# Stores on ScalarE's DMA queue, one tile late, in a batched outer-product kernel

## The chip, the cores and the metric

The kernel runs on one core of a Trainium2 chip. The metric is the device time of one execution in microseconds (us). Engines are named as in the profile: PE is the tensor engine's matmul, PEld its weight load, DVE is VectorE, ACT is ScalarE, POOL is GpSimd, SP is SyncE. A q behind the name (SPq, ACTq) is that engine's sequencer, which among other things issues DMAs.

## The reference

```
x: [8, 12, 512, 64] f32,  y: [8, 12, 512, 64] f32
out = einsum('bhtc,bhsc->bhts', x, y)      # [8, 12, 512, 512] f32
```

For each of the 96 pairs of batch and head, a 512 x 64 matrix is multiplied by the transpose of another. 25.17 MB are read and 100.66 MB written.

## The kernel before

**Tiling.** The 96 heads form NG = 12 groups of 8. A group's x and y are loaded as two transfers of 1 MB each into the two halves of one slot, a tile of 128 partitions by 16 KB; the pool has SLOTS = 5 of these. An output tile is 128 partitions by 8 x 512 f32, 2 MB, and takes a slot of the same pool. There are 4 x 12 = 48 output tiles ("results" 0 to 47), each stored by one 2 MB transfer.

**Steps.** `load(g)` takes a slot and issues the two loads on SP. `compress(g)` casts the group to bf16 into tiles that are kept: all of x on ACT, y in four quarters, of which two go to DVE, one to POOL and the last to ACT. After this the slot is free. `mix(i)` rearranges x of half a group into one of two tiles that were set to zero once, and `transposes(i)` makes the two matmul operands of that half with DVE's 32 x 32 transposes. `result(o)` takes a slot, runs eight matmuls into three PSUM tiles (of 3, 3 and 2 banks), and copies them into the slot: the first two on ACT, the third on DVE. It then records a piece of work for a later result (a `transposes` after an even result; after an odd one, a `mix` for one of the half-groups 6 to 23, with one quarter of it on ACT; half-groups 0 to 5 are mixed on POOL in the first loop), and returns a function that issues the store.

**Order.** The order is written out by hand: on each engine the instructions stand as the program calls them. The first loop runs over the 12 groups. It casts each group as its load lands, issues the remaining loads (group 10 after group 6 is cast, group 11 after group 8), and fits in results 0, 1 and 2 after groups 5, 7 and 9, whose store functions it only collects. After the loop, all 12 groups are cast. The program then calls the three collected stores, and goes on with results 3 to 47, storing each at once.

**Queues.** All loads and all stores are issued by SP, in program order: the 24 loads first, the 48 stores behind them. Each issue waits on SP for what it needs: a load for its slot to be free, a store for the copies on ACT and DVE. Since SP does nothing else, it is free to wait. It issues store 0 right after the last load, at 54.14 us, while ACT is still casting groups 9 to 11 until 65.94 us.

Of the kernel before, what the change touches and what calls it, by code (L numbers as in the profile page):

```python
# [1 line left out]

# [4 lines left out]


@with_exitstack
def kernel(  # L10
    ctx: ExitStack,
    tc: tile.TileContext,
    x: bass.AP,
    y: bass.AP,
    out: bass.AP,
):

    nc = tc.nc
    B, H, T, C = x.shape
    _, _, S, _ = y.shape
    P = 128  # L30
    G = 8
    Q = P // G
    R = T // Q
    NG = B * H // G
    K = 8
    E = R // K
    D = 32
    SLOTS = 5
    fp32 = mybir.dt.float32
    bf16 = mybir.dt.bfloat16  # L40
    u32 = mybir.dt.uint32
    COPY = mybir.ActivationFunctionType.Copy
    assert C == 2 * D and S == T and R == D and Q * 2 == D

    xv = x.rearrange("b h t c -> (b h t c)").rearrange("(g p n) -> g p n", p=P, n=R * C)
    yv = y.rearrange("b h t c -> (b h t c)").rearrange("(g p n) -> g p n", p=P, n=R * C)
    ov = out.rearrange("b h t s -> (b h t s)").rearrange(
        "(o u h q n) -> o h q u n", u=2, h=2, q=Q * E, n=K * S
    )

    const = ctx.enter_context(tc.tile_pool(name="const", bufs=1))
    kept = ctx.enter_context(tc.tile_pool(name="kept", bufs=NG))
    slots = ctx.enter_context(tc.tile_pool(name="slots", bufs=SLOTS))
    tpool = ctx.enter_context(tc.tile_pool(name="tpool", bufs=3))
    pm3pool = ctx.enter_context(tc.tile_pool(name="pm3psum", bufs=2, space=bass.MemoryType.PSUM))
    pm2pool = ctx.enter_context(tc.tile_pool(name="pm2psum", bufs=1, space=bass.MemoryType.PSUM))

    loaded, inputs, mixed, made = {}, {}, {}, {}
    zeroed = [const.tile([P, K * E * D], u32, name=f"xb{half}") for half in range(2)]
    in_front = [nc.vector, nc.gpsimd, nc.vector, nc.scalar]  # L60
    behind = [nc.vector, nc.gpsimd, nc.scalar, nc.vector]
    FIRST = NG // 2

    def copy(engine, dst, src):
        if engine is nc.scalar:
            nc.scalar.activation(dst, src, COPY)  # L66
        else:
            engine.tensor_copy(dst, src)  # L68

    def slot():  # L70
        return slots.tile([P, K * S], fp32, name="slot")

    def load(g):
        both = slot()
        nc.sync.dma_start(both[:, :R * C], xv[g])  # L75
        nc.sync.dma_start(both[:, R * C:], yv[g])
        loaded[g] = both

    def compress(g):

        both = loaded.pop(g)
        xk = kept.tile([P, R, C], bf16)
        nc.scalar.activation(xk.rearrange("p r c -> p (r c)"), both[:, :R * C], COPY)  # L83
        inputs[g] = xk
        ys = both[:, R * C:].rearrange("p (r c) -> p r c", c=C)
        for half in range(2):
            yb = kept.tile([P, R // 2 * D], u32, name=f"yb{half}")
            yv2 = yb.bitcast(bf16).rearrange("p (j c w) -> p j w c", j=R // 2, w=2)
            for ch in range(2):
                copy(  # L90
                    in_front[2 * half + ch],
                    yv2[ch * 64:(ch + 1) * 64],
                    ys[half * 64:(half + 1) * 64, :, ch * D:(ch + 1) * D].rearrange(
                        "p (j w) c -> p j w c", w=2
                    ),
                )
            mixed[2 * g + half] = yb

    def mix(i, engines, halves=(0, 1)):

        g, half = divmod(i, 2)
        xk = inputs[g]
        xv2 = zeroed[half].bitcast(bf16).rearrange("p (k e c u) -> p k e c u", k=K, e=E, u=2)
        for ch in halves:
            for u in range(2):
                lo = half * 64 + u * D
                copy(
                    engines[2 * ch + u],
                    xv2[(2 * ch + u) * D:(2 * ch + u + 1) * D, :, :, :, u],
                    xk[lo:lo + D, :, ch * D:(ch + 1) * D].rearrange("p (e k) c -> p k e c", k=K),  # L110
                )

    def transposes(i):
        xb, yb = zeroed[i % 2], mixed.pop(i)
        xT = tpool.tile([P, K * D * E], u32)
        nc.vector.transpose(  # L116
            xT.rearrange("p (k r e) -> p k e r", k=K, e=E),
            xb.rearrange("p (k e c) -> p k e c", k=K, e=E),
        )
        yT = tpool.tile([P, D * R // 2], u32)  # L120
        nc.vector.transpose(  # L121
            yT.rearrange("p (r j) -> p j r", r=D), yb.rearrange("p (j c) -> p j c", c=D)
        )
        made[i] = (xT.bitcast(bf16).rearrange("p (k h m) -> p k h m", k=K, h=2), yT.bitcast(bf16))

    def result(o):

        i, h = divmod(o, 2)
        xT, yT = made[i]
        otf = slot()  # L130
        ot = otf.rearrange("p (r s) -> p r s", s=S)
        for k, n in ((0, 3), (3, 3), (6, 2)):
            pm = (pm3pool if n == 3 else pm2pool).tile([P, n, S], fp32, name=f"pm{n}")
            for j in range(n):
                nc.tensor.matmul(  # L135
                    pm[:, j, :], xT[:, k + j, h, :], yT[:, h * S:(h + 1) * S], start=True, stop=True
                )
            copy(nc.scalar if n == 3 else nc.vector, ot[:, k:k + n, :], pm)
        if h == 0 and i + 2 < 2 * NG:
            transposes(i + 2)  # L140
        elif h == 1 and FIRST <= i + 4 < 2 * NG:
            mix(i + 4, behind)
        return lambda: nc.sync.dma_start(ov[i, h], otf)  # L143

    with tc.manual_schedule():
        for g in range(SLOTS):
            load(g)
        nc.vector.memset(zeroed[0], 0.0)  # L148
        nc.gpsimd.memset(zeroed[1], 0.0)  # L149
        stores = []  # L150
        for g in range(NG):
            compress(g)
            mix(g // 2, [nc.gpsimd] * 4, (g % 2,))
            if g in (2, 4):
                transposes(g // 2 - 1)
            if g < 5:
                load(g + SLOTS)
            elif g in (5, 7, 9):
                stores.append(result(len(stores)))
            elif g in (6, 8):  # L160
                load(g // 2 + 7)
        for store in stores:
            store()
        for o in range(len(stores), 4 * NG):
            result(o)()


# [1 line left out]
_INS = ['x', 'y']  # L169
_OUTS = [((8, 12, 512, 512), 'float32')]  # L170


# [23 lines left out]
```

## Time and profile before

| | us |
|---|---|
| median of 3 runs (301.9 to 302.25) | 301.96 |
| the profiled execution | 302.28 |
| its span, first to last instruction | 300.5 |
| DVE busy | 189.2 |
| ACT busy | 198.1 |
| PE busy | 148.4 |
| POOL busy | 82.0 |
| one store issue on SP, median of 48 | 0.539 |
| ACT waiting for a store to land, 33 times | 51.3 |

The profile page describes one execution on the chip. A row of the list of groups reads: line, engine, operation, output<-input with shapes, count; then busy time in all and mean ns of one; then idle time of the engine just before, and what ended it. The strip cuts the span into 40 slices of 7.5 us; each digit is a busy share in tenths. "DMA to landing" is the time from an issue's start until its data has arrived and the semaphore says so. A line of the timeline reads: start, duration, engine, line, operation. Matmul ends are modelled. An engine's idle time costs nothing unless the end of the program hangs on it.

### The profile page before, as it was taken

Reading aid. Unit: us, or ns where it says so; the run is one execution under the profiler, and the core shown is the slowest. Engines: PE = TensorE matmul, PEld = TensorE weight load, DVE = VectorE, ACT = ScalarE, POOL = GpSimd, SP = SyncE. Lnnn points to the kernel's source line nnn. Section 1 sums busy time; section 2 is a strip of 40 time slices with the busy share of each in tenths; the row PEclk is TensorE's granted clock in tenths of the full one; section 3 lists DMA queues with packets and bytes.
Section 4 is the critical chain, followed back from the end, with each engine's and each line's share of the span. In section 5 each row is a group of like instructions: output and inputs, shape, how many; then the busy total and the mean of one; then the engine's idle time right before and its main releaser. Section 6 shows DMA issues by size and latency. Waiting matters only on the chain.

```text
span 300.5 us, 1448 instructions
## 1 busy us (share of the span) xinstructions
PE 148.4 (49%) x384; PEld 47.6 (16%) x384; DVE 189.2 (63%) x157; ACT 198.1 (66%) x139; POOL 82.0 (27%) x59
## 2 busy tenths in 40 slices
PE   0004044228647573765675567666476767475000
PEld 0001011003212121221121122212121222121000
DVE  1568998895997669666767576757765775313000
ACT  4666598999976867686668676777677664647000
POOL 1899989991211011101110111011101100000000
PEclk9999575577997659567756855756955765955555
DMA  7999999999999999999999999999999999999994
GB/s 282 429 424 421 423 422 422 423 435 434 423 434 426 425 438 430 425 443 421 433 436 425 432 430 425 438 430 423 442 423 430 441 421 430 432 422 427 436 425 181
DMA packets 10377, 125.93 MB, mean 419 GB/s; under 512 B 1152, under 2 KB 1152, under 8 KB 1152
## 3 DMA queue, kind: packets, MB, share of 16 engines
q1 hardware_dynamic: 10368, 125.83, 98.7%
q8 instruction: 3, 0.05, 0.1%
q14 instruction: 6, 0.05, 0.0%
HBM read 25.17 MB, written 100.66 MB: 419 GB/s over the span
## 4 chain that ended last, share of the span: by engine, by line
DMA 65%; ACT 15%; DVE 7%; PE 3%; issue 1%; ACTq 1%; SPq 0%; DVEq 0%
DMA out_dram<-slot 56%; ACT slot L66 11%; DMA slot<-in_y_dram 9%; DVE yb L68 4%; PE pm L135 3%; ACT xk L83 3%; DVE xT L116 2%; ACT yb L66 2%; DVE slot L68 1%; DVE yT L121 1%; ACTq L191 0%; SPq L75 0%; ACTq L66 0%; DVEq L68 0%; SPq L143 0%
## 5 line engine op out<-in xcount | busy, mean ns | idle before, releaser
L135 PE MATMUL pm<-yT,xT 128*128 128x512 bf16 x384 | 148.4, 537 | 127.3 <-ACT slot L66 102.2
L66 ACT ACTIVATE slot<-pm 128x1536 f32<-128x1536 f32 x96 | 133.9, 1448 | 65.8 <-DMA out_dram<-slot 51.3
L68 DVE COPY slot<-pm 128x1024 f32<-128x1024 f32 x48 | 58.8, 1225 | 72.0 <-PE pm L135 54.4
L68 POOL COPY xb<-xk 32x1024 bf16<-32x1024 bf16 x42 | 62.2, 1482 | 145.4 <-DVE xT L116 144.3
L135 PEld LDWEIGHTS <-xT 128*128 128x128 bf16 x384 | 47.6, 124 | 227.2 <-issue 193.9
L116 DVE STREAM_TRANSPOSE xT<-xb 128x1024 uint32<-128x1024 uint32 x24 | 49.3, 2054 | 0.7
L68 DVE CAST yb<-slot 64x1024 bf16<-64x1024 f32 x24 | 35.2, 1466 | 13.5 <-DMA slot<-in_y_dram 13.2
L83 ACT ACTIVATE xk<-slot 128x2048 bf16<-128x2048 f32 x12 | 22.9, 1910 | 9.6 <-DMA slot<-in_x_dram 9.4
L68 DVE COPY xb<-xk 32x1024 bf16<-32x1024 bf16 x36 | 26.3, 731 | 0.5
L121 DVE STREAM_TRANSPOSE yT<-yb 128x512 uint32<-128x512 uint32 x24 | 25.0, 1041 | 0.0
L66 ACT ACTIVATE xb<-xk 32x1024 bf16<-32x1024 bf16 x18 | 24.1, 1338 | 0.4
L68 POOL CAST yb<-slot 64x1024 bf16<-64x1024 f32 x12 | 18.8, 1567 | 8.1 <-DMA slot<-in_y_dram 7.4
L66 ACT ACTIVATE yb<-slot 64x1024 bf16<-64x1024 f32 x12 | 15.9, 1324 | 3.6 <-DMA slot<-in_y_dram 3.4
L83 ACT ACT_TABLE_LOAD x1 | 1.3, 1283 | 0.7 <-PEq L180 0.7
L148 DVE MEMSET xb<- 128x1024 uint32 x1 | 0.9, 912 | 1.0 <-PEq L180 1.0
L149 POOL MEMSET xb<- 128x1024 uint32 x1 | 1.0, 952 | 0.3 <-POOLq L180 0.3
L180 POOL MEMSET const-float32-0.0<- 128x1 f32 x1 | 0.1, 98 | 0.2 <-issue 0.2
L180 POOL MEMSET const-float32-1.0<- 128x1 f32 x1 | 0.1, 98 | 0.0
L180 POOL MEMSET const-bfloat16-1.0<- 128x1 bf16 x1 | 0.1, 98 | 0.0
L180 POOL MEMSET const-uint8-127<- 128x1 uint8 x1 | 0.1, 98 | 0.0
## 6 DMA issues: line engine op xcount, KB each, us to landing
out_dram<-slot SPq DMA_DIRECT2D x48, 2048.0 KB, 21.7
slot<-in_x_dram SPq DMA_DIRECT2D x12, 1024.0 KB, 17.5
slot<-in_y_dram SPq DMA_DIRECT2D x12, 1024.0 KB, 19.3
```

Of the source, the lines that this page charges most:

```text
L66: nc.scalar.activation(dst, src, COPY)
L68: engine.tensor_copy(dst, src)
L83: nc.scalar.activation(xk.rearrange("p r c -> p (r c)"), both[:, :R * C], COPY)
L116: nc.vector.transpose(xT.rearrange("p (k r e) -> p k e r", k=K, e=E), xb.rearrange("p (k e c) -> p k e c", k=K, e=E),)
L121: nc.vector.transpose(yT.rearrange("p (r j) -> p j r", r=D), yb.rearrange("p (j c) -> p j c", c=D))
L135: nc.tensor.matmul(pm[:, j, :], xT[:, k + j, h, :], yT[:, h * S:(h + 1) * S], start=True, stop=True)
L148: nc.vector.memset(zeroed[0], 0.0)
L149: nc.gpsimd.memset(zeroed[1], 0.0)
L180: nc = _bacc.Bacc("TRN2", target_bir_lowering=False, num_devices=1)
```

## The change

The stores are issued by ACT instead of SP, and each one stands behind the copies of the next result. In detail:
- In `result`, the returned function calls `nc.scalar.dma_start` in place of `nc.sync.dma_start`.
- After the loop over the groups, stores 0 and 1 are called, and store 2 is kept back. Each further result is recorded first, with its two copies and, after an odd result, its quarter of a mix on ACT, and then the store of the result before it is called. The last store is called at the end.

On ACT, stores 0 and 1 now stand behind the casts of group 11 and ahead of the copies of result 3. SP issues the 24 loads and nothing else. No copy, matmul or transpose is added, removed or moved against another.

```diff
@@ -140,7 +141,7 @@
             transposes(i + 2)
         elif h == 1 and FIRST <= i + 4 < 2 * NG:
             mix(i + 4, behind)
-        return lambda: nc.sync.dma_start(ov[i, h], otf)
+        return lambda: nc.scalar.dma_start(ov[i, h], otf)
 
     with tc.manual_schedule():
         for g in range(SLOTS):
@@ -159,10 +160,13 @@
                 stores.append(result(len(stores)))
             elif g in (6, 8):
                 load(g // 2 + 7)
-        for store in stores:
-            store()
-        for o in range(len(stores), 4 * NG):
-            result(o)()
+        done = len(stores)
+        while len(stores) > 1:
+            stores.pop(0)()
+        for o in range(done, 4 * NG):
+            stores.append(result(o))
+            stores.pop(0)()
+        stores.pop()()
```

## The prediction

> **What bounds the kernel now.** I read the strip of 40 slices and the queues first, then the chain, then the few microseconds in which the kernel turns from loading to storing.
>
> ```profile
> DMA  7999999999999999999999999999999999999994
> GB/s 282 429 424 421 423 422 422 423 435 434 423 434 426 425 438 430 425 443 421 433 436 425 432 430 425 438 430 423 442 423 430 441 421 430 432 422 427 436 425 181
> q1 hardware_dynamic: 10368, 125.83, 98.7%
> DMA 65%; ACT 15%; DVE 7%; PE 3%; issue 1%; ACTq 1%; SPq 0%; DVEq 0%
> L66 ACT ACTIVATE slot<-pm 128x1536 f32<-128x1536 f32 x96 | 133.9, 1448 | 65.8 <-DMA out_dram<-slot 51.3
> out_dram<-slot SPq DMA_DIRECT2D x48, 2048.0 KB, 21.7
> ```
>
> The 16 DMA engines are busy in every slice but the first and last. One queue carries all 125.83 MB and fills 98.7% of the span. ACT, at 66%, waits for stores to land, not the other way round. The chain names compute engines for a third of the span, but a chain follows releases: under those pieces the strip still shows DMA at 9. So the test of the change is one question: **do the DMA engines stay fed?** Every microsecond in which they stand dry comes out at the end.
>
> A store takes 21.7 us to land, but two tiles together take 9.89 us (ACT's copies of every second tile start at 206.44 and 216.33), 4.94 each: about four stores are queued at any time. A late store is therefore harmless wherever several others are queued. The place to look is where none can be: the end of the loads.
>
> ```profile
> L76 SPq DMA_DIRECT2D slot<-in_y_dram x1: 423/423/423, 53.7 to 53.7; - x1
> DMA to landing us min/median/max: 9.1/9.1/9.1
> ...
> L143 SPq DMA_DIRECT2D out_dram<-slot x1: 653/653/653, 54.1 to 54.1; - x1
> DMA to landing us min/median/max: 13.6/13.6/13.6
> ```
>
> The last load (the y of group 11) is issued at 53.67 (timeline of SP) and lands at 62.8. Store 0 is issued at 54.14, straight behind it, and lands at 67.7, just 4.9 us, one store's time, after that load. No gap at all: before's stores 0 and 1 lie in the queue while the last loads still move, and store 2 joins at 59.4.
>
> ```profile
> 61.33 1.32 ACT L66 ACTIVATE yb<-slot 64x1024 bf16<-64x1024 f32 x1
> 62.68 1.91 ACT L83 ACTIVATE xk<-slot 128x2048 bf16<-128x2048 f32 x1
> 64.62 1.32 ACT L66 ACTIVATE yb<-slot 64x1024 bf16<-64x1024 f32 x1
> ...
> L66 ACTq EVENT_SEMAPHORE  x1: 17/17/17, 62.8 to 62.8; - x1
> ```
>
> The last two ACT rows are group 11: its x cast starts at 62.68, its y cast at 64.62. The fourth line is the first wait of ACT's sequencer (ACTq) for the copies of result 3, which follow that y cast in program order. It stands at 62.8, exactly when y of group 11 lands, and not at 65.94, when the cast ends. The same is seen for group 9: its y lands at 32.97 + 19.9 = 52.87, its cast starts only at 55.18, and the sequencer's next wait is recorded at 52.9. So ACT's sequencer passes a cast as soon as the cast's own semaphore has come.
>
> **What the Trainium skill says.** "DMA: Bandwidth & Descriptors", section "Issuing engines are not separate DMA queues": the issuing engine changes nothing but who spends the issue time; all DMAs share the same 16 engines. The trace of before has one queue at 98.7%, so it can't test this, but it leaves no bandwidth for a second queue to find. "Perfetto Trace Analysis", section "Per-engine timelines": an ACT instruction is pushed into a wait queue and the sequencer goes on, while a DMA instruction is executed by the sequencer itself. The two readings at 62.8 and 52.9 agree, with the limit that the sequencer stood still until the last pushed instruction's semaphore came. The first-named page, section "Latency and other measured facts", gives about 0.6 us to the first byte on this path; the trace's only DMA on an empty queue took longer (below).
>
> **The change part by part.**
>
> Removed: the 48 store issues on SP and SP's waits for them. SP has nothing else to do then. Worth 0.
>
> Loads: same issues and waits on SP, and in before no store stands ahead of a load. 0.
>
> Added to ACT: 48 issues, 0.54 us each on SP (538 ns the least, 653 the longest, of 48). In two tiles ACT has four copies of 1.45 and one mix of 1.34, 7.1 us of 9.89, so 2.8 are free; two issues take 1.1. Not on the path: 0. If that cover is gone, see rival C.
>
> Stores issued later: store o-1 goes out once the sequencer has passed the copies (and on every second tile the mix) of tile o. Tile o starts copying when store o-5 has landed. At that moment o-4, o-3 and o-2 are still queued, 3 x 4.94 = 14.8 us of work less the landing lag. Store o-1 follows at most 2.9 + 1.34 + 0.54 = 4.8 us later, with 2 us until it moves: some 8 us are left. 0 in the steady part and at the end; the time from issue to landing should fall by 4 us or so, which is not time saved. The added wait, for VectorE's copy of tile o-1, holds back ACT's copies of tile o+1. But in before VectorE's copy ends at 202.93 and ACT's copies of that tile at 204.27; one tile later it is long done. 0.
>
> **Stores 0 and 1: the price.** In the built order of ACT, both stand behind the casts of group 11 and ahead of the copies of result 3, and carry no semaphore wait. They can't be issued before the y cast of group 11 is passed, and that needs the last load to have landed. So the DMA engines, which run loads and nothing else until then, fall dry once:
> - last byte to landing. The first load is issued at 0.74, its packets begin at 2.7 (windows of 0.1 us: share 0.00 up to 2.70, then 0.89), it lands 4.9 after issue at 5.6, and loads land 2.48 apart (ACT's first x and y casts, 5.64 and 8.13, start on landings). 4.9 - 2.0 - 2.5 = 0.4 us.
> - landing to issue: the sequencer's wait at 62.80 against 62.77: 0.03 us.
> - issue to first packet: 2.0 us by that first load, 0.6 by the skill's figure. I take 2.0: it is measured here, and ACT's queue will be as unused as SP's was. The first load was cold in other ways too, so both ends stay: 0.6 to 2.0.
>
> Sum 0.4 + 0.0 + 2.0 = **2.4 us**, at the low end 1.0. Upwards, the mixed stretch of loads and stores is lost as well (438 GB/s in 60 to 62 us against 423 before): at most 0.3 us; and slower engines may start later: up to 3.2 in all. Is there a second dry spell? Store 1 follows 0.6 us behind store 0; together 9.9 us of work from about 64.8 to 74.7. Store 2 needs only that the copies of result 3 be passed (they start at 65.96 in before) and goes out by 68. Store 3 by about 71, behind copies that end at 71.9 in before. No.
>
> Nothing can win the time back, since the rest is DMA at 430 GB/s to the end. The profiled run took 302.28 for a span of 300.5; with 2.4 it becomes 304.7, span 302.9. The median of the runs lies 0.3 lower, at 301.96: forecast **304.4 us**.
>
> **The rivals.**
> - A: ACT issues a DMA only when its engine has finished what stands before it. Then store 0 waits for the y cast's end, 65.96 instead of 62.80: 3.2 more, 5.6 in all, 307.5. For it: no trace here shows a DMA on ACT. Against: the reading at 62.8, and store 3 on carry a semaphore wait for ACT's own copies, which would be idle if the order held by itself.
> - B, the other side, not slower: stores on a queue of their own, three deep instead of four, move faster. 100.66 MB at 430 GB/s are 234 us; the dry 2.4 us are paid back from 434.4 GB/s on. The skill's ceiling, 435 ("DMA: Bandwidth & Descriptors", "Bandwidth"), allows 231.4, so at best 301.7. For it: single slices reach 443. Against: the mean is the same in all of the store phase and nothing in it waits for the queue. A dry spell of only 0.6 us or less, below what can be seen, falls here too.
> - C: issuing from ACT costs much more than from SP, so that ACT becomes the bound. It decides from 1.4 us an issue (2.8 free over two); at 2.0 it costs 1.2 us for each of some 21 pairs, 25 us: about 329. Against: nothing in the issue itself, the same form of DMA, points to triple the price.
>
> **How the numbers follow.** Forecast 0.63, A 0.17, B 0.15, C 0.05. The range, 302.4 to 307.8, covers the forecast's 303.0 to 305.2 and A and the edge of B; it leaves C and most of B out. What can be told from no change is 0.2%, 0.6 us. B splits into 0.07 faster and 0.07 the same; 0.86 slower.
>
> **What would show it.** In the changed profile: the strip's DMA row dips in one slice around 60 to 68 us; the stores' queue shows some 80% and the loads' 20%; store 0 is issued near 62.8 and lands near 70.1 (67.7 before); the median from issue to landing drops to 17 or 18 us; ACT's waits for stores do not grow; GB/s after 70 us are 430 again. A is right if store 0 goes out at 66. The prediction is wrong if the DMA row shows no dip, if there are several, or if the rate after 70 us has moved by more than 0.5%.

## The result, and the profile after

The changed kernel takes 304.37 us (304.36 to 304.45), against 302.11 us for the kernel before beside it: a ratio of 1.0073, interval 1.0057 to 1.0088. It is 2.3 us slower. The profiled execution took 304.38 us with a span of 302.6, 2.1 us more than before in both.

From the page of the changed kernel: the strip's DMA row and rate, the queues, the first lines of the chain, ACT's copies with their idle time, and the stores' issues.

```profile
DMA  7999999979999999999999999999999999999996
GB/s 289 423 427 419 421 428 418 421 323 416 435 426 416 429 435 420 431 431 425 422 435 425 418 435 422 425 435 419 426 435 425 418 444 414 425 438 422 422 442 266
q10 hardware_dynamic: 6912, 100.67, 78.4%
q1 hardware_dynamic: 3456, 25.17, 20.1%
DMA 73%; ACT 9%; DVE 6%; PE 2%; issue 1%; ACTq 1%; SPq 0%; DVEq 0%
L67 ACT ACTIVATE slot<-pm 128x1536 f32<-128x1536 f32 x96 | 134.0, 1448 | 67.9 <-DMA out_dram<-slot 58.7
out_dram<-slot ACTq DMA_DIRECT2D x48, 2048.0 KB, 19.2
```

One digit in 40 has changed in the middle of the DMA row: the ninth slice, 60.5 to 68.1 us, is at 7 with 323 GB/s. The loads (q1) and the stores (q10) now have a queue each, and their shares add to 98.5%, of a longer span.

The next lines are from the timeline of ACT around the turn from loads to stores (start, duration, engine, line), followed by the first store's issue with its time to landing, and by windows of the same stretch. The last three figures of a window are the PE clock, the DMA share and GB/s; a packet is counted in the window in which it begins.

```profile
62.60 1.91 ACT L84 ACTIVATE xk<-slot 128x2048 bf16<-128x2048 f32 x1
62.74 2.66 ACTq L144 DMA_DIRECT2D out_dram<-slot  x3
64.53 1.33 ACT L67 ACTIVATE yb<-slot 64x1024 bf16<-64x1024 f32 x1
65.88 1.45 ACT L67 ACTIVATE slot<-pm 128x1536 f32<-128x1536 f32 x1
...
L144 ACTq DMA_DIRECT2D out_dram<-slot x1: 645/645/645, 62.7 to 62.7; - x1
DMA to landing us min/median/max: 6.8/6.8/6.8
```

```profile
62.00:64.00 2.00, 0.00 (x0) 0.00 (x0) 1.97 (x2) 1.98 (x2) 1.94 (x2) 1.00 0.00 0
64.00:66.00 2.00, 0.00 (x0) 0.00 (x0) 1.99 (x2) 1.95 (x3) 1.94 (x2) 0.71 1.14 475
80.00:290.00 210.00, 118.69 (x316) 38.78 (x320) 128.98 (x113) 137.15 (x99) 22.45 (x17) 0.72 1.01 427
```

From 62 to 64 us no packet of data begins. The last load lands at 62.7 (issued at 53.6, 9.1 to landing), ACT's sequencer issues store 0 at 62.74, while the x cast of group 11 is still running and its y cast has not begun, and packets appear at 64.0. Store 0 lands at 62.74 + 6.8 = 69.5 us, 1.8 us later than before (67.7). The kernel before had 455 GB/s in the same two microseconds:

```profile
62.00:64.00 2.00, 0.00 (x0) 0.00 (x0) 1.97 (x2) 1.98 (x2) 1.94 (x2) 1.00 1.07 455
80.00:290.00 210.00, 124.80 (x323) 39.67 (x320) 128.63 (x113) 136.29 (x99) 22.52 (x17) 0.67 1.01 430
```

At the other end, the last store lands at 280.4 + 21.4 = 301.8 us, against 278.3 + 21.4 = 299.7. From store 0's landing to the last one's are 232.3 us in the changed kernel and 232.0 in the one before, which is alike within the rounding of these figures. So nearly all of the loss is there before the store phase begins.

### The profile page after: what moved, and what is told of

Its sections match the earlier page's. It is cut to its first block, busy times and chain, and to the rows that moved or that the text cites. A ratio compares the mean times of both kernels' runs of the same rounds, so it can differ in the third digit from the quotient of the medians.

```text
span 302.6 us, 1418 instructions
## 1 busy us (share of the span) xinstructions
PE 142.7 (47%) x377; PEld 46.8 (15%) x384; DVE 189.6 (63%) x157; ACT 198.2 (66%) x139; POOL 81.9 (27%) x59
## 3 DMA queue, kind: packets, MB, share of 16 engines
q1 hardware_dynamic: 3456, 25.17, 20.1%
HBM read 25.17 MB, written 100.66 MB: 416 GB/s over the span
## 4 chain that ended last, share of the span: by engine, by line
DMA 73%; ACT 9%; DVE 6%; PE 2%; issue 1%; ACTq 1%; SPq 0%; DVEq 0%
DMA out_dram<-slot 64%; DMA slot<-in_y_dram 9%; ACT slot L67 5%; DVE yb L69 4%; ACT xk L84 2%; PE pm L136 2%; ACT yb L67 1%; DVE xT L117 1%; ACTq L144 1%; DVE slot L69 1%; DVE yT L122 1%; SPq L76 0%; ACTq L67 0%; DVEq L69 0%; ACT xb L67 0%
## 5 line engine op out<-in xcount | busy, mean ns | idle before, releaser
L136 PE MATMUL pm<-yT,xT 128*128 128x512 bf16 x377 | 142.7, 524 | 134.1 <-ACT slot L67 109.2
L67 ACT ACTIVATE slot<-pm 128x1536 f32<-128x1536 f32 x96 | 134.0, 1448 | 67.9 <-DMA out_dram<-slot 58.7
L69 POOL COPY xb<-xk 32x1024 bf16<-32x1024 bf16 x42 | 62.1, 1479 | 147.3 <-DVE xT L117 146.1
L136 PEld LDWEIGHTS <-xT 128*128 128x128 bf16 x384 | 46.8, 122 | 229.5 <-issue 194.0
## 6 DMA issues: line engine op xcount, KB each, us to landing
out_dram<-slot ACTq DMA_DIRECT2D x48, 2048.0 KB, 19.2
slot<-in_y_dram SPq DMA_DIRECT2D x12, 1024.0 KB, 19.2
```

The costliest lines, as they stand in the source:

```text
L136: nc.tensor.matmul(pm[:, j, :], xT[:, k + j, h, :], yT[:, h * S:(h + 1) * S], start=True, stop=True)
```

## The experiments

Theory D is that of the prediction: the loss is the one dry spell of the DMA engines where the loads end. Rival Q is that the loss is spread over the store phase, because of ACT's queue, the late issue, or fewer stores in flight. In all diffs below, the function that `result` returns takes the queue as an argument (ACT's if none is given).

### 1. Stores 0 and 1 back on SP

```diff
         while len(stores) > 1:
-            stores.pop(0)()
+            stores.pop(0)(nc.sync)
```

> Stores 0 and 1 are issued by SP behind the loads, as in the kernel before; all others by ACT, one tile late, as in the changed kernel. Theory D (the loss is the one dry spell of the DMA engines at the end of the loads): no dry spell, 302.2 us, and store 0 lands near 67.7. Rival Q (the loss is spread over the store phase: the ACT queue, the late issue, or the shorter queue costs about 0.05 us a store): 46 of the 48 stores still pay, 304.3 us.

Measured: 301.72 us (ratio to the kernel before 0.9982, 0.9975 to 0.9989). Two of 48 stores moved back, and all of the loss is gone. Store 0 lands at 67.7 again, and the engines are fed in the two microseconds that were dry:

```profile
62.00:64.00 2.00, 0.00 (x0) 0.00 (x0) 1.97 (x2) 1.98 (x2) 1.94 (x2) 0.50 1.06 451
```

Q falls. That the time is even 0.5 us under the kernel before was not expected; experiments 7 to 10 are about that.

### 2. The mirror image: three stores on ACT, 45 on SP

```diff
         for o in range(done, 4 * NG):
             stores.append(result(o))
-            stores.pop(0)()
-        stores.pop()()
+            if o == done:
+                stores.pop(0)()
+            stores.pop(0)(nc.sync)
```

> The mirror image: stores 0, 1 and 2 are issued by ACT behind the casts of group 11, as in the changed kernel; stores 3 to 47 by SP, each as soon as it is ready. Theory D: the dry spell from 62.0 to 64 us is there, 304.4 us, although 45 stores are issued as before. Rival Q: 302.2 us.

Measured: 304.47 us (1.0074, 1.0059 to 1.0089), as D said. The dry stretch is there again:

```profile
62.00:64.00 2.00, 0.00 (x0) 0.00 (x0) 1.96 (x3) 1.98 (x2) 1.94 (x2) 0.50 0.04 16
```

With three late stores the whole loss is back, and it doesn't matter that the other 45 are issued as before.

### 3. Only store 2 on SP

```diff
-        while len(stores) > 1:
+        stores.pop(2)(nc.sync)
+        while stores:
             stores.pop(0)()
         for o in range(done, 4 * NG):
             stores.append(result(o))
-            stores.pop(0)()
+            if o > done:
+                stores.pop(0)()
```

> The changed kernel, with store 2 alone moved to SP, where it is issued when its copies are done, near 59.4 us, ahead of stores 0 and 1. Theory D: one queued store of 4.9 us covers the spell until stores 0 and 1 come at 62.7, so no dry slice and 302.2 us. Rival Q, or a cost of being late of stores 0 and 1 themselves: 304.3 us.

Measured: 301.69 us (0.998, 0.9969 to 0.999). Stores 0 and 1 go out as late as in the changed kernel, at 62.9 us, and it costs nothing, since store 2 was issued at 59.4 and fills the engines meanwhile (414 GB/s from 62 to 64 us). So what costs is not that a given store is late but that nothing at all is queued.

### 4. The dry spell made longer

```diff
         done = len(stores)
+        for o in range(done, done + 2):
+            stores.append(result(o))
         while len(stores) > 1:
             stores.pop(0)()
-        for o in range(done, 4 * NG):
+        for o in range(done + 2, 4 * NG):
```

> The changed kernel, with stores 0, 1 and 2 placed behind the copies of result 4 (with store 3), where ACT's sequencer passes near 70.3 us instead of 62.7. Theory D: the dry spell grows by 7.5 us and comes out at the end one for one, 311.9 us. Rival R (a dry spell is partly won back, since more copies are done ahead when the stores start): under 310 us.

Measured: 311.86 us (1.0317, 1.03 to 1.0334). From the windows of this run, and its first store:

```profile
64.00:66.00 2.00, 0.00 (x0) 0.00 (x0) 1.99 (x2) 1.95 (x3) 1.94 (x2) 0.50 0.00 0
66.00:68.00 2.00, 0.58 (x2) 0.26 (x2) 2.00 (x2) 2.00 (x2) 1.94 (x2) 0.50 0.00 0
68.00:70.00 2.00, 2.00 (x7) 0.56 (x5) 0.23 (x1) 1.68 (x2) 0.31 (x1) 0.50 0.00 0
...
L144 ACTq DMA_DIRECT2D out_dram<-slot x1: 644/644/644, 70.2 to 70.2; - x1
...
DMA to landing us min/median/max: 6.9/6.9/6.9
```

The engines stand dry until past 71 us. Store 0 is issued 7.5 us later than in the changed kernel (70.25 against 62.74), and the time is 7.5 us longer: one for one, though result 3 had been copied and result 4 begun by the time the stores went out. Nothing is won back: from there on the DMA engines are the bound again, and ACT only waits longer for stores (64.2 us in all against 58.7).

### 5. Stores 0 and 1 between the two casts of group 11

```diff
         inputs[g] = xk
+        if g == NG - 1:
+            stores.pop(0)()
+            stores.pop(0)()
```

(The rest of this diff is cut: the list `stores` is made before `compress`, and the two stores are no longer called after the loop.)

> The changed kernel, with stores 0 and 1 moved on ACT from behind the y cast of group 11 to between its x cast and its y cast. ACT's sequencer passes the x cast when that x has landed, near 60.3 us. Theory D: store 0 is issued at 60.4, its packets can start at 61.7, no dry spell, 301.7 to 302.2 us. Rival A (a DMA on ACT goes out only when the engine has finished what stands before it, the x cast at 64.5): still over 306 us.

Measured: 301.87 us (0.9984, 0.9977 to 0.9991). The timeline of ACT in this run:

```profile
59.46 1.91 ACT L86 ACTIVATE xk<-slot 128x2048 bf16<-128x2048 f32 x1
60.38 1.29 ACTq L149 DMA_DIRECT2D out_dram<-slot  x2
61.40 1.33 ACT L67 ACTIVATE yb<-slot 64x1024 bf16<-64x1024 f32 x1
62.76 1.91 ACT L86 ACTIVATE xk<-slot 128x2048 bf16<-128x2048 f32 x1
```

In the program the two issues stand behind the x cast of group 11, the last line. They go out at 60.38, 2.4 us before that cast starts and while the one of group 10 is running: when x of group 11 has landed (issued at 53.3, 7.0 us to landing). This shows at a second place the rule that the forecast rested on, and it is also the cheapest repair of the changed kernel: the same queue, with the two issues moved ahead by one instruction.

### 6. The dry spell without any DMA on ACT

```diff
-        while len(stores) > 1:
-            stores.pop(0)()
+        late, stores = stores, []
         for o in range(done, 4 * NG):
-            stores.append(result(o))
-            stores.pop(0)()
-        stores.pop()()
+            result(o)(nc.sync)
+            for store in late:
+                store(nc.sync)
+            late = []
```

> No DMA on ACT at all: every store is on SP, as in the kernel before, but store 3 stands ahead of stores 0, 1 and 2, so that SP waits with all of them until the copies of result 3 end, near 68.8 us. Theory D: a dry spell from 62.0 to some 70.0 us, 6.1 us longer than in the changed kernel, 310.5 us. Rival (the loss has to do with ACT's queue): about 302 us, since all 48 stores are on SP.

Measured: 310.37 us (1.0265, 1.0251 to 1.0279). The first store is issued at 68.65 us, 5.9 later than in the changed kernel, and the time is 6.0 longer. From the windows of this run:

```profile
66.00:68.00 2.00, 0.66 (x2) 0.26 (x2) 2.00 (x2) 2.00 (x2) 1.94 (x2) 0.50 0.00 0
68.00:70.00 2.00, 2.00 (x6) 0.63 (x5) 0.14 (x1) 1.68 (x2) 0.23 (x1) 0.50 0.14 57
```

With every store on SP a dry spell costs the same, microsecond for microsecond, so ACT's queue is not the cause of the loss.

### 7 to 10. The half microsecond gained without a dry spell

Experiment 7, SP and ACT in turn:

> Even stores on SP as soon as they are ready, odd ones on ACT one tile late, store 0 behind the loads as before: no dry spell. Where do the 0.5 us come from that the kernels with 46 or 47 stores on ACT and no dry spell gained on the kernel before (301.7 against 302.2)? If from ACT's queue or from two queues being used at once: 301.7 or less. If from the shorter queue of stores in flight (19.3 us to landing against 21.7): about 302.0. If it is chance: 302.2.

Experiment 8, on ACT but not late:

> Stores 0, 1 and 2 on SP, the others on ACT, each behind its own copies instead of those of the next result: four in flight again. Theory D: no dry spell, so 301.7 to 302.2 us; 302.2 if the small gain came from the shorter queue, 301.7 if it came from ACT's queue. Rival H (ACT loses time by standing in front of its own store, waiting for VectorE's copy): the wait is 0 to 1 us a tile and lies within ACT's idle time, but if it did count, up to 20 us more.

Experiment 9, ACT at the turn only:

> Stores 0 to 2 on SP, 3 to 9 on ACT, 10 to 47 on SP, each as soon as it is ready. No dry spell in any theory. It places the small gain of 0.5 us that the kernel with stores 3 to 47 on ACT showed (301.75 against 302.33): if it is made at the turn from loads to stores, where two queues meet, 301.75; if it is spread over the store phase, 302.2; if it is made at the end, 302.3.

Experiment 10, ACT at the end only:

> Stores 0 to 39 on SP, the last eight on ACT, each as soon as it is ready. If the small gain is made at the turn from loads to stores: 302.3. If spread over the store phase: 302.2. If at the end, where the last engine is some 2 us behind the others: 301.75.

The edits are in the loop after the groups; the lines ahead of and behind it are cut here. Ahead of it, stores 0 and 2 (experiment 7) or 0 to 2 (the others) are called with `nc.sync`, and store 1 of experiment 7 on ACT:

```diff
# experiment 7 (`stores` is empty when the loop begins)
-            stores.append(result(o))
-            stores.pop(0)()
+            store = result(o)
+            for held in stores:
+                held()
+            stores = []
+            if o % 2:
+                stores = [store]
+            else:
+                store(nc.sync)
# experiment 8
-            stores.append(result(o))
-            stores.pop(0)()
+            result(o)()
# experiment 9 (the same two lines go)
+            result(o)(nc.scalar if o < 10 else nc.sync)
# experiment 10 (the same two lines go)
+            result(o)(nc.scalar if o >= 40 else nc.sync)
```

| stores | us | ratio to before (interval) |
|---|---|---|
| 7: SP and ACT in turn | 302.3 | 1.0 (0.9992 to 1.0008) |
| 8: 3 to 47 on ACT, not late | 301.75 | 0.9983 (0.9975 to 0.9991) |
| 9: 3 to 9 on ACT | 302.27 | 1.0 (0.9992 to 1.0009) |
| 10: 40 to 47 on ACT | 302.28 | 1.0001 (0.9992 to 1.0009) |

Experiment 8 has as many stores in flight as the kernel before (21.7 us from issue to landing, the same as there) and still gains, so the gain is not from the shorter queue. It also settles rival H: that ACT stands behind its own copies costs no time, and issuing a tile late wasn't needed for it. Experiments 9 and 10 show that the gain is made neither at the turn nor at the end alone; 7, that it isn't there when the two queues share the stores. What remains is that it was seen only where ACT's queue carried 45 or more of the 48 stores and there was no dry spell. Why stays open. Between experiment 2 and the changed kernel, which both have the dry spell, no such gain is seen (1.0074 and 1.0073), but the two intervals are too wide to rule out one of 0.5 us.

The kernels of experiments 1, 3, 5 and 8 beat both the kernel before and the changed one, by about 0.2% and 0.8 to 0.9%; experiment 3 was the lowest at 301.69.

## Why the prediction was right

**The dry spell, as the only loss.** Right. It was the one place found where no other store could be queued; experiments 1 to 3 turn the loss off, on and off again with it, and 4 and 6 show that it comes out one for one. In the profiled executions the time from store 0's landing to the end is nearly the same: 304.38 - 69.5 = 234.9 us in the changed kernel, 311.87 - 77.1 = 234.8 in experiment 4, 310.1 - 75.5 = 234.6 in experiment 6, and 302.28 - 67.7 = 234.6 in the kernel before.

**The sequencer passes the casts; rival A.** Right: store 0 goes out at 62.74, not 65.9, and experiment 5 shows it at a second place. The evidence had been two 17 ns records of waits, at 62.8 and 52.9, and it was worth 3.2 us of the forecast.

**The terms of the 2.4 us.** The mechanism was right and the sum a little large, but its terms are less good than the sum. Landing to issue is 0.0, as said. By the trace's records of single packets, the 16 engines end their last packet of the loads between 61.95 and 62.26 us, 62.1 in the mean. That is 0.6 us ahead of the landing, not 0.4. Packets appear 1.3 us after the issue, neither the 2.0 that was taken nor the 0.6 that was kept as the lower end. The 2.0 came from the first load of the kernel, and was taken because ACT's queue would be as unused as SP's was then. That is not what sets this lag: in experiment 6 SP's queue has carried 24 loads, and its first packet on dry engines also follows the issue by 1.3 us (68.65, then 69.9 to 70.0). Why the first load takes 0.7 more is not shown. So an engine stands dry for 2.0 us in the mean, and the profiled execution is 2.1 longer.

The 0.3 that was set aside for the mixing of loads and stores was a misreading. The 438 GB/s of the window before 62 us counts whole packets that begin there and end later. By the packet records the two kernels have moved 25.15 MB (before) and 25.17 MB (changed) by 62 us, so nothing was lost. That the forecast of 304.4 us met 304.37 so closely is in part luck: the spell was 0.4 shorter than the sum, and the base of 301.96, from three runs, was 0.15 below the 302.11 beside the changed kernel.

**Steady part, tail and rival C.** Right that nothing is late there: an issue takes ACT 0.547 us, and experiment 8 shows that even without the delay ACT has room. Two expectations failed without costing time. The median from issue to landing fell to 19.2 us, not to 17 or 18: I had let store o-1 wait until the copies of tile o were done, but the sequencer passes them as it passed the casts, so a store goes out soon after the first of these copies starts (at 208.74 against 208.66, and 204.21 against 203.81). And ACT's waits for stores grew, from 51.3 to 58.7 us, without a cost in time.

**Rival B and the rate.** The mean rate after the turn is 427 GB/s, 0.7% under the 430 of before, more than the 0.5% that I had named as a sign of error. By that sign the prediction would have been wrong; it was a poor gauge. The mean is over 16 engines, and the end is set by the last. A share of 0.06 is one engine's. The windows near the end, first of before, then of after, show that in the kernel before most engines end early and a last one late, and that in the changed kernel they end closer together:

```profile
296.00:297.00 1.00, 0.00 (x0) 0.00 (x0) 0.00 (x0) 0.00 (x0) 0.00 (x0) 0.50 0.31 131
297.00:298.00 1.00, 0.00 (x0) 0.00 (x0) 0.00 (x0) 0.00 (x0) 0.00 (x0) 0.50 0.08 33
298.00:299.00 1.00, 0.00 (x0) 0.00 (x0) 0.00 (x0) 0.00 (x0) 0.00 (x0) 0.50 0.04 16
```

```profile
298.00:299.00 1.00, 0.00 (x0) 0.00 (x0) 0.00 (x0) 0.00 (x0) 0.00 (x0) 0.50 0.85 360
299.00:300.00 1.00, 0.00 (x0) 0.00 (x0) 0.00 (x0) 0.00 (x0) 0.00 (x0) 0.50 0.81 344
300.00:301.00 1.00, 0.00 (x0) 0.00 (x0) 0.00 (x0) 0.00 (x0) 0.00 (x0) 0.50 0.08 33
```

A lower mean and a last engine that ends in step with the others go together here; landings are what count. The spell is not what brings this about, for experiment 5, which has none, shows the same:

```profile
80.00:290.00 210.00, 122.87 (x325) 39.60 (x323) 128.60 (x113) 136.77 (x99) 22.50 (x17) 0.69 1.01 427
296.00:297.00 1.00, 0.00 (x0) 0.00 (x0) 0.00 (x0) 0.00 (x0) 0.00 (x0) 0.50 1.15 492
297.00:298.00 1.00, 0.00 (x0) 0.00 (x0) 0.00 (x0) 0.00 (x0) 0.00 (x0) 0.50 0.31 131
```

The rate is 430 in every kernel whose store 0 is issued at 54.1 us, and 427 or 428 in every one whose first store comes at 59.4 or later. Why stays open. Rival B did not come true: what ACT's queue brought where there is no spell is 0.5 us, a fifth of what would have paid the loss back, and its cause is not known.

## What to carry to other kernels

Where the DMA engines are the bound, ask of a moved transfer not how late it is but whether anything else is queued when it is late. The answer can be no at a single place, here where the loads end and the stores begin, and there each microsecond of standing dry was a microsecond at the end. A DMA on ACT's queue waited for the semaphores of the instructions ahead of it, not for their execution, so placing it one instruction earlier can matter (here 2.5 us between the changed kernel and experiment 5), and one queued store closed the gap (experiment 3). Compare landings of the first and the last transfer rather than mean rates, which hide how far apart the engines end.

## What the runs showed of the hardware that was not expected

- The third and later of several stores issued in a row took longer to issue, on either engine. On ACT the last of the three that begin at 62.74 took 1.145 us, and with four in a row (experiment 4) the longest took 1.351, against 0.547 for a store by itself. On SP (experiment 6) the longest took 1.364, against 0.539. In experiment 3, where one store was already queued, the second of two took 1.372.
- On empty engines a 2 MB store lands 6.8 to 6.9 us after its issue, from ACT (the changed kernel, experiments 2 and 4) and from SP (experiment 6) alike, some 1.9 us more than the 4.94 that one takes in a full queue.
- With 45 to 48 stores on a queue other than that of the loads and no dry spell, the time was about 0.5 us of 302 lower (experiments 1, 3, 5 and 8), with no cause found.
